# Restacking rotated queries and keys: SBUF-to-SBUF copies replaced by a write to DRAM and a read back

## The chip, the cores and the metric

The kernel runs as one program on 1 core of one Trainium2 chip. The metric is the device time of one execution in microseconds (us). Five engines work side by side, each through its own in-order queue: TensorE (PE, matrix products; PEld is its weight load), VectorE (DVE), ScalarE (ACT), GpSimd (POOL), and SyncE (SP), which here does nothing but issue transfers. The transfers run on 16 DMA engines.

## The reference, cut to what matters

Two requests (x_prompt and x_sample, 512 tokens by 1024 each) go through the same two encoder layers and a last norm. One layer computes:

```
h    = rmsnorm(x) * (1 + scale) + shift          # scale, shift, gate from silu(c) @ w_ada
proj = h @ w_in                                  # 1024 -> qa ka va ga qb kb vb gb
A: 8 heads x 64: rotary q, k; three centred windows (128,1) (512,4) (2048,16),
   merged by their softmax denominators; times silu(ga)
B: 4 heads, key 64, value 128: rotary q, k; two-directional retention with decay,
   RMS norm per head; times silu(gb)
x    = x + gate * (concat(A, B) @ w_out)
```

At 512 tokens every head is one 512 by 512 score matrix with a mask (A) or a decay table (B). Both need `q . k` over the 64 rotated elements of a head, and this is where the change lies.

## The kernel before, in words

**Precision.** A float32 operand is split into a rounded high part and a low part (`hi`, `lo`), and a product is taken as hi·hi + lo·hi + hi·lo. With a head of 64 and 128 rows in the array, q's two parts are stacked on the 128 partitions (a tile QS), and k's high part is stacked twice (KS), its low part twice (KL). One product QS by KS then gives (q_hi + q_lo)·k_hi, a second one QS by KL adds the low part of k.

**Projection and order.** `ITEMS` lists 20 projection items a layer: four of query/key pairs of A (PQK), two of B (RQK), values (PV, RV) and gates (G). The main loop (line 1267) runs through them in that order and issues their products on PE. Everything else is written as generators (tasks) that a planner (`Plan`, line 125) steps through: it keeps a clock for every engine, adds an estimated cost for each instruction, and takes a task's next step when its due time, the value it yields, has come on PE's clock. The planner runs while the program is built; its choices fix the order of every engine's queue. Buffers come from a heap of half tiles (`Heap`), PSUM banks from `Banks`; a step is also held until those it needs are free.

**A turn.** Each query/key item is done once for each request: (4 + 2) items by 2 requests by 2 layers make 24 turns, and a turn holds two heads. `rope` (line 851) does a turn: six DVE operations apply the rotation to two PSUM banks (tiles rc and rs, which hold for both heads the first and the second half of q and k, 32 rows each), ACT rounds the two results to `hi`, DVE subtracts to get `lo`. Then come the copies (lines 868 to 877): for each head four copies into QS, four into KS, four into KL, each of 32 partitions by 2 KB, 64 KB, from SBUF to SBUF. All 24 are one step of the task: nothing else can be put between them on SP. Their due time is 1.5 us before the last source is planned to be ready; the four source tiles are given back after the copies.

**Who uses the stacks.** `attn` (line 911) takes the stacks of an A turn, in turn order: scores on PE, mask and minimum on DVE, `soften` (line 934: exponential on ACT, scaling and splitting into pt on DVE), two DMA transposes a head (pt to pT, line 957, on SP), and the product with the values. `ret` (line 1044) takes those of a B turn: scores, decay on DVE, `halve`, products. The weights (`raw`, line 769) are loaded through the same SP queue, rounded by ACT to wH, and POOL subtracts to get wL.

**The planner's view of a transfer.** `note` (line 159) charges SP 650 ns for an SBUF-to-SBUF copy and 450 ns for one with DRAM (line 421), and lets the bytes run one after the other at a fixed rate. A write into part of a tile (fewer than 128 partitions) does not wait in the plan for the transfer before it into the same tile.

In the traces nearly every instruction has line 377, where the helper records it, so groups are told apart by the names of their tiles. The names rc, rs, th, sS, yr, KL and so on are those of whoever opened the buffer first, so copies into stacks appear also as `QS<-sS` or `sr<-rs`.

Of the kernel before, what the change touches and what calls it, by code (L numbers as in the profile page):

```python
# [10 lines left out]
F32 = mybir.dt.float32  # L11
F32R = mybir.dt.float32r
# [7 lines left out]
P = 128  # L20
# [16 lines left out]
K_STK = 6  # L37
# [87 lines left out]
class Plan:  # L125
# [31 lines left out]
        return 0.0 if t <= self.free[eng] else t  # L157

    def note(self, eng, cost, outs, ins, nbytes=0.0):
        part = eng == "SP" and outs[0].shape[0] < P  # L160
        outs = [k for a in outs for k in self.keys(a)]
        ins = [k for a in ins for k in self.keys(a)]
        start = self.free[eng]
        for k in ins:
            start = max(start, self.seen(eng, self.ready.get(k)))
        for k in outs:
            if not (part and self.last.get(k, (0.0, ""))[1] == "DMA"):
                start = max(start, self.seen(eng, self.last.get(k)))
        if self.dead.intersection(outs + ins):
            raise RuntimeError("use of a spare buffer")  # L170
        end = start + cost
        self.free[eng] = end
        if eng == "SP":
            self.dma = max(end + 650.0, self.dma) + nbytes
            end = self.dma + 770.0
            eng = "DMA"
        for k in outs:
            self.ready[k] = (max(end, self.ready.get(k, (0.0, ""))[0]), eng)
        for k in outs + ins:
            if end >= self.last.get(k, (0.0, ""))[0]:  # L180
                self.last[k] = (end, eng)
# [243 lines left out]
def trunk_kernel(  # L425
# [8 lines left out]
    plan = Plan()  # L434
    V, A, G, T, Q = (Engine(plan, n, e) for n, e in (("DVE", nc.vector), ("ACT", nc.scalar), ("POOL", nc.gpsimd),
                                                     ("PE", nc.tensor), ("SP", nc.sync)))
# [3 lines left out]
    dp = ctx.enter_context(tc.tile_pool(name="dp", bufs=1, space=bass.MemoryType.DRAM))  # L440
# [5 lines left out]
    H = Heap(plan, cp, "half", NHALF)  # L446
# [392 lines left out]
    def main_wide(pj, job, l, b):  # L839
        for t in range(TT):  # L840
            out = pj[:, t // 2, (t % 2) * 256:(t % 2) * 256 + 256]
            for k in range(KT):
# [5 lines left out]
                T.matmul(out, h, wl, start=False, stop=False)  # L848
                T.matmul(out, lo, wh, start=False, stop=(k == KT - 1))

    def rope(pj, c, s, res, b):
        yield lambda: plan.after("DVE", *pj)
        V.tensor_tensor(c[0], pj[0], cos, op=ALU.mult)
        V.tensor_tensor(s[0], pj[0], sin, op=ALU.mult)
        B_IN.free(pj[0])
        V.tensor_tensor(s[1], pj[1], sin, op=ALU.mult)
        V.tensor_tensor(c[0], c[0], s[1], op=ALU.subtract)
        V.tensor_tensor(c[1], pj[1], cos, op=ALU.mult)
        B_IN.free(pj[1])
        V.tensor_tensor(c[1], c[1], s[0], op=ALU.add)  # L860
        for t in (1, 0):
            yield lambda: plan.after("ACT", c[1 - t])
            A.activation(s[t].bitcast(F32R), c[1 - t], AF.Copy)
        hi, lo = (s[1], s[0]), c
        for t in range(2):
            yield lambda: plan.after("DVE", hi[t])
            V.tensor_tensor(lo[t], lo[t], hi[t], op=ALU.subtract)
        yield lambda: max(plan.at(*hi, *lo) - 1500.0, H.avail(1, 6, K_STK, "R"))
        out = []
        for h in range(2):  # L870
            qs, ks, kl = H.take(1, "QS"), H.take(1, "KS"), H.take(1, "KL")
            for i in range(4):
                Q.dma_start(qs[32 * i:32 * i + 32], (hi, lo)[i // 2][i % 2][32 * h:32 * h + 32])
            for t, src in ((ks, hi), (kl, lo)):
                for i in range(4):
                    Q.dma_start(t[32 * i:32 * i + 32], src[i % 2][64 + 32 * h:96 + 32 * h])
            out.append([x.bitcast(F32R) for x in (qs, ks, kl)])
        res["stk"][b] = out
        H.free(*c, *s)

    def turn(kind, i, b, pj, res):
        rs = res.setdefault((kind[0], i), {"stk": {}, "vv": {}})
        c, s = [H.take(1, "rc") for _ in range(2)], [H.take(1, "rs") for _ in range(2)]
        spawn(rope(pj, c, s, rs, b), front=True)
        if kind == "PQK":
            follow(attns, attn(i, b, rs))
# [361 lines left out]
    for l in range(DEPTH):  # L1248
# [8 lines left out]
        for ks in PIECES if l == 0 else ():  # L1257
            for idx in early:
                for t, pj in enumerate(early[idx]):
                    main_half(pj, jobs[idx], t, l, 0, ks)  # L1260
                if KT - 1 in ks:
                    kind, i = ITEMS[0][idx]
# [63 lines left out]
        for b in range(NB):  # L1326
            for t in range(TT):
# [8 lines left out]
                for c, (n0, n1) in enumerate(LAST if final else ((0, D),)):  # L1336
                    for n, k in enumerate(KORDER):
                        pump(lambda: plan.at(*yT[(k, b)], *wo[k]) if (k, b) in yT and k in wo else INF)
                        y, w = ([x.bitcast(F32R) for x in z] for z in (yT[(k, b)], wo[k]))
# [48 lines left out]
```

## Time and profile before

| | us |
|---|---|
| median of 3 runs | 1138.96 (1136.25 to 1142.01) |
| the profiled execution, its own time | 1141.08 |
| its span, first to last instruction | 1139.3 |
| PE busy | 1062.7 (93%) |
| DVE busy | 855.4 (75%) |
| ACT busy | 388.8 (34%) |
| POOL busy | 193.4 (17%) |
| mean granted TensorE clock | 0.973 of full speed |
| DMA, share of 16 engines | 55.0%, 163.55 MB |

Busy time is the sum of an engine's instructions. The span is cut into slices or stretches to see where an engine stands still; the chain of waits says which engine's work ended last at each moment. The 1.8 us between the span and the execution's own time lie outside the first and last instruction. A granted clock of 1.0 is 2.4 GHz, 0.5 is 1.2 GHz.

### The profile page before, as it was taken

Reading aid. Unit: us, or ns where it says so; the run is one execution under the profiler, and the core shown is the slowest. Engines: PE = TensorE matmul, PEld = TensorE weight load, DVE = VectorE, ACT = ScalarE, POOL = GpSimd, SP = SyncE. Lnnn points to the kernel's source line nnn. Section 1 sums busy time; section 2 is a strip of 40 time slices with the busy share of each in tenths; the row PEclk is TensorE's granted clock in tenths of the full one; section 3 lists DMA queues with packets and bytes.
Section 4 is the critical chain, followed back from the end, with each engine's and each line's share of the span. In section 5 each row is a group of like instructions: output and inputs, shape, how many; then the busy total and the mean of one; then the engine's idle time right before and its main releaser. Section 6 shows DMA issues by size and latency. Waiting matters only on the chain.

```text
span 1139.3 us, 15515 instructions
## 1 busy us (share of the span) xinstructions
PE 1062.7 (93%) x5443; PEld 838.8 (74%) x5443; DVE 855.4 (75%) x1664; ACT 388.8 (34%) x677; POOL 193.4 (17%) x84
## 2 busy tenths in 40 slices
PE   5979999999888989999999999999999999976997
PEld 3757787687766557777888878877887887854886
DVE  5577876688747979889447799589956986797555
ACT  6353314233124313454324333424234233334101
POOL 3052002010120201136000101102111012051000
PEclk9989999999989989999999999999999999987999
DMA  9804877316775756778322386336752477664232
GB/s 316 289 24 139 167 177 230 136 48 163 158 173 143 240 123 149 161 178 259 111 74 75 79 181 162 79 93 149 146 128 65 132 149 167 140 212 102 75 111 74
DMA packets 210429, 164.53 MB, mean 144 GB/s; under 512 B 162032, under 2 KB 172560, under 8 KB 210352
## 3 DMA queue, kind: packets, MB, share of 16 engines
q1 hardware_dynamic: 210352, 163.55, 55.0%
q8 instruction: 43, 0.70, 0.3%
q14 instruction: 34, 0.28, 0.1%
HBM read 79.59 MB, written 8.40 MB: 77 GB/s over the span
## 4 chain that ended last, share of the span: by engine, by line
PE 55%; DVE 25%; SPq 10%; DMA 4%; issue 3%; ACT 2%; POOL 0%; DVEq 0%; ACTq 0%; POOLq 0%
PE banks L377 55%; DVE pt L377 10%; SPq L377 10%; DVE sS L377 2%; DVE rc L377 2%; DVE yr L377 2%; DVE sm L377 1%; DVE th L377 1%; DMA wa<-in_w_ada_dram 1%; DVE hT L377 1%; DVE rsq L377 1%; DMA raw<-in_w_in_dram 1%; DVE sd L377 1%; DVE rs L377 1%; DVE b L377 1%
## 5 line engine op out<-in xcount | busy, mean ns | idle before, releaser
L377 PE MATMUL banks<-hT,wH 128*128 128x512 f32 x1536 | 487.3, 398 | 12.1 <-POOL hT L377 4.4
L377 PEld LDWEIGHTS banks<-hT,wH 128*128 128x128 f32 x1536 | 289.6, 191 | 92.0 <-issue 14.5
L377 PE MATMUL banks<-hT,wL 128*128 128x512 f32 x768 | 303.2, 395 | 3.7 <-POOL wL L377 3.7
L377 POOL TENSOR_TENSOR wL<-raw,wH 128x1024 fp32r<-128x1024 f32 x56 | 139.8, 2505 | 744.4 <-ACT wH L377 577.2
L377 PE MATMUL banks<-wo,yT 128*128 128x512 f32 (+1 forms) x744 | 170.7, 390 | 10.1 <-DVE yT L377 6.9
L377 PEld LDWEIGHTS banks<-hT,wL 128*128 128x128 f32 x768 | 146.5, 191 | 35.1 <-POOL wL L377 4.1
L377 PEld LDWEIGHTS banks<-wo,yT 128*128 128x128 f32 x744 | 139.0, 192 | 40.0 <-DVE yT L377 7.6
L377 PE MATMUL banks<-wH,hT 128*128 128x256 f32 x512 | 96.7, 285 | 0.5 <-ACT wH L377 0.5
L377 ACT ACTIVATE sS<-sS,sm 128x512 f32<-128x512 f32 x76 | 54.3, 715 | 88.2 <-DVE sm L377 78.4
L377 PEld LDWEIGHTS banks<-wH,hT 128*128 128x128 f32 x512 | 81.9, 193 | 2.0 <-ACT wH L377 0.7
L377 DVE SCALAR_TENSOR_TENSOR pt<-sS,sm,pt 128x512 f16<-128x512 f32 x76 | 75.5, 993 | 4.2 <-PE banks L377 1.1
L377 PE MATMUL banks<-wL,hT 128*128 128x256 f32 x256 | 73.1, 285 | 2.2 <-POOL wL L377 2.2
L377 ACT ACTIVATE wH<-raw 128x1024 fp32r<-128x1024 f32 x56 | 58.6, 1052 | 36.8 <-PE banks L377 19.0
L377 DVE CUSTOM_DVE_ANT_0 sS<-banks,tabs 128x512 f32<-128x512 f32 x76 | 49.1, 686 | 18.3 <-PE banks L377 15.9
L377 PE MATMUL banks<-sr,rv 128*128 128x512 f32 x166 | 49.1, 402 | 6.1 <-DVE sr L377 4.7
L377 DVE TENSOR_SCALAR pt<-sS,sm 128x512 f16<-128x512 f32 x76 | 51.4, 676 | 1.6 <-DMA KS<-rc 0.2
L377 PEld LDWEIGHTS banks<-wL,hT 128*128 128x128 f32 x256 | 49.4, 193 | 3.2 <-POOL wL L377 2.4
L377 DVE TENSOR_TENSOR res<-banks,gb 128x512 f32<-128x512 f32 (+1 forms) x33 | 22.1, 670 | 39.4 <-PE banks L377 39.4
L377 POOL TENSOR_TENSOR wo<-rawo,wo 128x1024 fp32r<-128x1024 f32 x16 | 41.2, 2596 | 57.6 <-PE banks L377 29.6
L377 PE MATMUL banks<-pT,vn 128*64 128x512 f16 x384 | 45.8, 383 | 1.6 <-DMA pT<-pt 1.1
L377 ACT ACTIVATE sq<-xr 128x1024 bf16<-128x1024 f32 (+2 forms) x15 | 14.2, 944 | 87.9 <-issue 43.2
L377 PE MATMUL banks<-wa,siluT 128*32 128x128 f32 (+1 forms) x384 | 33.0, 406 | 10.9 <-DMA wa<-in_w_ada_dram 7.9
(326 smaller groups left out, 1384.5 us busy)
## 6 DMA issues: line engine op xcount, KB each, us to landing
raw<-in_w_in_dram SPq DMA_DIRECT2D x56, 512.0 KB, 4.3
wa<-in_w_ada_dram SPq DMA_DIRECT2D x48, 512.0 KB, 4.9
rawo<-in_w_out_dram SPq DMA_DIRECT2D x16, 512.0 KB, 4.5
QS<-rs SPq DMA_DIRECT2D x88, 64.0 KB, 2.0
KL<-rc SPq DMA_DIRECT2D x88, 64.0 KB, 2.0
KS<-rs SPq DMA_DIRECT2D x66, 64.0 KB, 2.0
x1d<-xr SPq DMA_DIRECT2D x8, 512.0 KB, 2.8
xr<-x1d SPq DMA_DIRECT2D x8, 512.0 KB, 4.1
```

Source lines behind the costliest of these rows:

```text
L377: r = fn(*args, **kw)
```

## The change

A turn gets a scratch tile of 1 MB in DRAM, 128 rows by (half, part, 512). Each of the four source tiles is written to it whole, 128 partitions by 2 KB, 256 KB, as a step of its own with a due time 0.7 us before that tile is planned to be ready. The four source tiles are given back right after the writes. One more step, due 0.5 us before the scratch is planned to have landed, reads six stacks back, 256 KB each: QS as 128 rows in a run, KS and KL as 64 rows of which each is read twice. The rows of a stack come in another order than before, the same for q and k. In the planner, writes to a scratch tile don't wait for one another.

```diff
     def note(self, eng, cost, outs, ins, nbytes=0.0):
-        part = eng == "SP" and outs[0].shape[0] < P
+        part = eng == "SP" and (outs[0].shape[0] < P or outs[0].tensor.name.startswith("stk"))
...
-        yield lambda: max(plan.at(*hi, *lo) - 1500.0, H.avail(1, 6, K_STK, "R"))
+        nstk[0] += 1
+        rd = dp.tile([P, 2, 2, 512], F32, name=f"stk_dram{nstk[0]}")
+        for i, x in enumerate((*hi, *lo)):
+            yield lambda: plan.at(x) - 700.0
+            Q.dma_start(rd[:, i % 2, i // 2, :], x)
+        H.free(*c, *s)
+        yield lambda: max(plan.at(rd) - 500.0, H.avail(1, 6, K_STK, "R"))
         out = []
         for h in range(2):
-            qs, ks, kl = H.take(1, "QS"), H.take(1, "KS"), H.take(1, "KL")
-            for i in range(4):
-                Q.dma_start(qs[32 * i:32 * i + 32], (hi, lo)[i // 2][i % 2][32 * h:32 * h + 32])
-            for t, src in ((ks, hi), (kl, lo)):
-                for i in range(4):
-                    Q.dma_start(t[32 * i:32 * i + 32], src[i % 2][64 + 32 * h:96 + 32 * h])
-            out.append([x.bitcast(F32R) for x in (qs, ks, kl)])
+            q, k = rd[32 * h:32 * h + 32], rd[64 + 32 * h:96 + 32 * h]
+            srcs = [q.rearrange("p j w n -> (p j w) n")]
+            srcs += [k[:, :, w, :].rearrange("p j n -> (p j) n")[:, None, :].to_broadcast([64, 2, 512]) for w in range(2)]
+            ts = [H.take(1, n) for n in ("QS", "KS", "KL")]
+            for t, x in zip(ts, srcs):
+                Q.dma_start(t, x)
+            out.append([t.bitcast(F32R) for t in ts])
         res["stk"][b] = out
-        H.free(*c, *s)
```

## Rows read from the trace of the kernel before

**Rows 1.** The page, span in 40 slices: busy tenths of PE, DVE; granted clock.

```profile
PE   5979999999888989999999999999999999976997
DVE  5577876688747979889447799589956986797555
PEclk9989999999989989999999999999999999987999
```

**Rows 2.** Stretches: length; busy us of PE, PEld, DVE, ACT, POOL; clock; DMA share; GB/s.

```profile
80.00:280.00 200.00, 197.42 (x986) 152.75 (x985) 144.13 (x262) 58.18 (x106) 29.06 (x12) 0.99 0.55 147
280.00:360.00 80.00, 67.81 (x386) 52.36 (x386) 53.25 (x86) 26.36 (x45) 12.99 (x5) 0.91 0.71 164
360.00:460.00 100.00, 91.59 (x412) 65.51 (x411) 87.70 (x169) 32.87 (x69) 12.79 (x5) 0.95 0.67 172
500.00:520.00 20.00, 17.46 (x78) 13.04 (x74) 19.75 (x16) 11.32 (x16) 15.00 (x6) 0.91 0.70 178
640.00:1000.00 360.00, 355.56 (x1812) 290.81 (x1811) 287.71 (x523) 126.12 (x234) 56.32 (x23) 1.00 0.57 130
1000.00:1040.00 40.00, 22.60 (x94) 16.36 (x93) 38.11 (x50) 18.55 (x33) 19.93 (x8) 0.75 0.68 190
```

**Rows 3.** Chain that ended last, 280 to 360, then 1000 to 1040: shares by line.

```profile
by line: SPq L377 33.1%; PE banks L377 13.2%; DMA pT<-pt 10.1%; issue 6.4%; DVE pt L377 6.0%; DVE sm L377 4.3%; DVE rc L377 4.0%; POOL wL L377 3.6%; DVE sr L377 3.3%; DMA QS<-rc 2.5%; DMA KS<-b 2.4%; DVE yr L377 2.4%; DVE rsq L377 1.7%; DVE
...
by line: DVE pt L377 57.9%; issue 13.8%; DVE sm L377 9.5%; DVE y L377 5.0%; DVE th L377 4.9%; DVE sS L377 4.7%; PE banks L377 2.0%; DVE yT L377 1.5%; DVE rsq L377 1.5%; DVEq L377 0.6%; ACT sS L377 0.5%; DVE yr L377 0.1%; ACTq L377 0.0%
```

**Rows 4.** Timeline of SP: start, duration; the last two turns' copies and what stands between.

```profile
922.48 0.54 SPq L377 DMA_DIRECT2D sr<-rs  x1
...
937.00 0.59 SPq L377 DMA_DIRECT2D KS<-rc  x1
937.68 4.69 SPq L377 DMA_TRANSPOSE pT<-pt  x2
942.55 1.03 SPq L377 DMA_DIRECT2D raw<-in_w_in_dram  x2
944.59 3.40 SPq L377 DMA_TRANSPOSE vn<-vt  x1
948.03 1.21 SPq L377 DMA_DIRECT2D sr<-rs  x2
```

**Rows 5.** Timeline of DVE: a pt half done, and the last turn's rotation done.

```profile
926.57 0.75 DVE L377 SCALAR_TENSOR_TENSOR pt<-yr,sm,pt 128x512 f16<-128x512 f32 x1
...
933.19 1.29 DVE L377 TENSOR_TENSOR rc<-rc,rs 128x512 f32<-128x512 f32 x2 [1.40 <-ACT rs L377]
```

**Rows 6.** Transfers into QS: SP time min/median/max ns, first and last start; us to landing.

```profile
L377 SPq DMA_DIRECT2D QS<-rs x88: 507/588/1932, 76.2 to 960.8; - x88
...
DMA to landing us min/median/max: 1.9/2.0/6.0
```

**Rows 7.** The same for the 512 KB writes to a DRAM scratch and reads from it.

```profile
L377 SPq DMA_DIRECT2D x1d<-xr x8: 326/326/327, 534.5 to 611.2; - x8
L377 SPq DMA_DIRECT2D xr<-x1d x8: 319/376/423, 1022.0 to 1117.0; - x8
...
DMA to landing us min/median/max: 2.8/3.4/4.4
```

**Rows 8.** The same for outputs, 256 KB twice among nine.

```profile
L377 SPq DMA_DIRECT2D out_dram<-res x9: 337/338/382, 1062.8 to 1136.0; - x9
...
DMA to landing us min/median/max: 2.9/3.1/3.4
```

**Rows 9.** The same for the transposes of pt.

```profile
L377 SPq DMA_TRANSPOSE pT<-pt x64: 1679/2408/4582, 105.3 to 1039.6; - x64
...
DMA to landing us min/median/max: 4.3/5.0/6.5
```

**Rows 10.** Stretches: copies alone; then the last two 256 KB writes to DRAM alone.

```profile
262.00:270.00 8.00, 8.00 (x37) 6.64 (x36) 4.11 (x14) 3.63 (x9) 0.00 (x0) 1.00 0.44 105
...
1136.00:1137.00 1.00, 0.00 (x0) 0.00 (x0) 0.00 (x0) 0.00 (x0) 0.00 (x0) 0.67 0.57 215
1137.00:1138.00 1.00, 0.00 (x0) 0.00 (x0) 0.00 (x0) 0.00 (x0) 0.00 (x0) 0.50 0.83 309
```

**Rows 11.** Timeline of SP and chain, 298 to 350: copies, loads behind them, a product's wait.

```profile
308.10 0.59 SPq L377 DMA_DIRECT2D KS<-rc  x1
308.79 1.03 SPq L377 DMA_DIRECT2D raw<-in_w_in_dram  x2
...
308.79 1.14 DMA raw<-in_w_in_dram
318.37 2.91 POOL wL L377
...
341.78 1.93 DMA KS<-b
```

**Rows 12.** Timeline of DVE: two pt operations of one kind in the last stretch.

```profile
1006.51 0.75 DVE L377 SCALAR_TENSOR_TENSOR pt<-sS,sm,pt 128x512 f16<-128x512 f32 x1
...
1013.54 2.71 DVE L377 SCALAR_TENSOR_TENSOR pt<-sS,sm,pt 128x512 f16<-128x512 f32 x1
```

More of the change, by code (lines that the diff above doesn't have):

```diff
@@ L849, in main_wide @@
                 T.matmul(out, lo, wh, start=False, stop=(k == KT - 1))
+    nstk = [0]
     def rope(pj, c, s, res, b):
```

## The prediction

> **What bounds the kernel now.** First the page's slices [rows 1]: PE is at nine tenths or more in most of them, so the span is a full PE with holes, and the question is which holes belong to the copies. The table of stretches [rows 2] says where they are. I count a hole as PE's idle time plus what the lower granted clock takes, at most (1 - clock) times the stretch, an upper bound because the mean clock also covers idle time. 280 to 360: 80 - 67.8 = 12.2 idle and 0.09 x 80 = 7.2 of clock, 19.4 together. 360 to 460: 8.4 + 5.0 = 13.4. 500 to 520: 2.5 + 1.8 = 4.3. 640 to 1000: 4.4, clock 1.00. 1000 to 1040: 17.4 + 10.0 = 27.4. Sum 68.9 us: that is all the change can win, since before 80 us no turn is copied but for a few issues, and after 1040 there are no turns.
>
> Then the chain of waits in the two worst stretches [rows 3]. In 280 to 360 SP's queue holds 33% of it, the transposes behind it 10%, PE 13%: this stretch belongs to SP. In the timeline [rows 11] the last copy of a turn goes out at 308.10, the weight load right behind it at 308.79, and POOL's wL, for which PE then waits, comes only at 318.4; at 341.78 a copy itself is what the chain waits on. DVE is not the cause there: busy 53.3 of 80. In 360 to 460 it is (87.7 of 100). In 1000 to 1040 DVE's pt holds 58% and SP nothing, DVE is busy 38.1 of 40. There DVE also runs slowly: POOL is busy 19.9 of 40 [rows 2], and the same pt operation takes 2.71 us in place of 0.75 [rows 12].
>
> **What the change removes, adds and moves.** Removed: 24 copies a turn at 0.59 us (median) on SP. In the timeline [rows 4] one turn runs from 922.48 to 937.00 + 0.59 = 937.59: 15.1 us, 0.63 a copy with the gap. With the landing of 2.0 [rows 6] a stack is complete 17.1 us after its first copy. 24 turns hold SP for 24 x 15.1 = 362 us.
>
> Added: 4 writes at 0.33 us [rows 7, 8] = 1.3 us, a wait for the last one to land, and 6 reads at 0.38 [rows 7] = 2.3 us. Both issue times are of transfers of 128 partitions with DRAM on one side, as these are. The landing of 256 KB is not shown alone; from below it is 2.0, the 64 KB copy; from above 4.4, the slowest 512 KB to or from scratch [rows 7], and 6.0 where other transfers are queued ahead [rows 6]. I take 3.0, the nine outputs [rows 8], two of which are of just this size. So SP is held 1.3 + 3.0 + 2.3 = 6.6 us a turn (5.6 to 9.6), and 8.5 are freed, 24 x 8.5 = 204 us of SP. The plan may put other issues into the wait; I count none. Behind the waiting read stand SP's next issues: weights, transposes, the next turn's writes; for these wait ACT's wH, then POOL's wL, then PE, and the products with the values. They stood behind 15.1 us of copies before.
>
> The stack: all four sources ready, the last write 0.3, landing 3.0, six reads 2.3, landing of the last 4.0 (between 3.0 and 4.4, six together being more than one): 9.6 us in place of 17.1, so 7.5 earlier.
>
> The bytes grow from 24 x 64 KB = 1.57 MB to 10 x 256 KB = 2.62 MB a turn. What that costs the 16 engines: copies alone move 105 GB/s at a share of 0.44, 239 at full share; writes of 2 KB rows to DRAM move 215 at 0.57 and 309 at 0.83, 375 at full share [rows 10]. So 6.6 us of the engines' time before and 7.0 after if the reads run like the writes, 11.0 if they run like the copies. I take 7.0, DRAM rows of the same length; at 11.0 the share grows by 24 x 4.4 / 1139 = 9 points over 55, most of it where transposes also run.
> The Trainium skill (DMA: Bandwidth & Descriptors, Specifications) has transfers at line rate from 512 B a row on, with a ceiling of 435 GB/s. By that both kinds would cost the same per byte, 3.6 us before and 6.0 after, an estimate from that page. It would add 2.4 us a turn beside the transposes and take perhaps a third of the gain, 1118; the trace does not agree, its copies stay at 239.
>
> Moved: source buffers come free after the writes, some 10 us sooner, and a turn holds six halves of the heap at its reads where it held ten. Cost nothing; a gain only where a projection waits for buffers, which I don't count. Each write is its own step, and waits on SP at most the planned 0.7 us for ACT or DVE; the one step before waited up to 1.5. No cost either way. DVE, ACT, POOL and PE keep all their instructions, and the weight products keep their order; where scores and DVE work stand among them the plan will change.
>
> **The sum**, by stretches. 280 to 360: SP is the chain, and it shrinks to less than half of its length; DVE has 27 us idle there. Two thirds of 19.4, 13. 360 to 460: DVE-bound, but some of its work can move forward into those 27 idle us; half of 13.4, 7. 500 to 520: the same, half, 2. 640 to 1000: half, 2. 1000 to 1040: worked from the last two turns [rows 4, 5]. The last rotation ends at 933.2 + 1.3 = 934.5, its first copy goes out at 948.0, 13.5 later, because SP was in the turn before until 937.6 and then in two transposes, a load and another transpose (10.4 us). The pt half ready at 927.3 was transposed at 937.7. With 6.6 in place of 15.1 for the turn before, the last one starts at 948.0 - 8.5 = 939.5 and is complete 9.6 + 1.0 later, 950 in place of 948.0 + 15.9 + 2.0 = 966. That is 16 us, in which DVE is a fifth idle (287.7 of 360), and it lets the last scores spread out. But POOL's subtractions stay beside the end. Half of 27.4, 14.
> Gain 13 + 7 + 2 + 2 + 14 = 38. Against it 4 us for a new hole: a new order of queues makes one somewhere, and PE lost 12.2 in a stretch of three or four of them, so 3 to 4 each. 1141.1 - 34 = 1107 against the profiled execution's own time; the median of the runs lies 2.1 below that: **1105**.
>
> **Rivals.**
> *All holes go*: SP was behind the DVE-bound stretches too, since late stacks made DVE idle first and full afterwards (53 of 80, then 88 of 100). For: this order of the stretches. Against: the POOL contention at the end, and the holes' clock part is an upper bound. 1141.1 - 68.9 - 2.1 = 1070. Chance 0.10.
>
> *The round trip is slow*: writes land behind transposes and weight loads in the same engines, and the in-order SP stands. Price: both landings at the 6.5 of the slowest transpose [rows 9]: held 1.3 + 6.5 + 2.3 = 10.1, stack complete after 0.3 + 6.5 + 2.3 + 6.5 = 15.6, so 5.0 of 8.5 and 1.5 of 7.5 remain. Some 40% of the 38 is left, 15: 1124. For: transposes and turns stand side by side [rows 4]. Against: scratch transfers never took over 4.4. It reaches 15.1, no gain, only at a landing of 11.5. Chance 0.14.
> The Trainium skill (DMA: Bandwidth & Descriptors, Latency and other measured facts) puts an access of HBM at 0.2 us and 2 us at high load, and calls its write receipt the slowest. By it a landing would be 3.0 + 1.8 = 4.8 under load, an estimate, and the time about 1113. The scratch rows (2.8 to 4.4) partly bear it out.
>
> *Hidden anyway*: the stretch 640 to 1000 has turns back to back and PE lost 4.4 in 360. If 280 to 360 only hands its holes on to DVE, full from 370 on, and the end stays with POOL, nothing is left: 1139. Chance 0.13.
>
> *Slower, by DVE's order*: stacks that come earlier put scores, masks and pt into DVE's in-order queue ahead of the rotations and gates that give PE its projection banks back. Place: 360 to 460, where DVE has 12 us to spare, and the turns of 760 to 840 in layer 1. It decides if more than those 12 us of attention move in there: then PE stands as it does at 1000 to 1040. Price: one more hole of 27.4 against a gain in 280 to 360 alone: 1141.1 + 27.4 - 13 - 2.1 = 1153. For: PE's waits inside full-DVE stretches exist already. Against: a score step is held while DVE's planned clock is more than 3 us ahead of PE's. Chance 0.16.
>
> **Numbers.** Forecast 0.47 (1090 to 1120), all holes 0.10, slow round trip 0.14, hidden 0.13, slower 0.16. Half a per cent, 5.7 us, is what a measurement of this kernel can tell from no change. Faster: 0.47 + 0.10 + 0.13 of the slow round trip = 0.70. Same: 0.13 + 0.01 = 0.14. Slower 0.16. Range: half of all holes lies below 1078; of the slower case half lies above 1148; 1078 to 1148 leaves out about 0.13, and I keep it, since the 27.4 may come in part only.
>
> **What would show it.** Right: SP's issues of a turn 3.6 us with a wait of 2 to 4 between writes and reads; landings under 4.4; SP's share of the chain in 280 to 360 under 15%, PE over 73 of 80 there; the last stack before 955, and PE idle near 9 in the last 40 us before the output products. Wrong: reads that wait over 6 us on SP; a DMA share over 64%; PE holes released by DVE in places where there were none; the end still 17 idle with DVE full, which would say that the stacks were not what made it late.

## The result, and the profile after

The changed kernel takes 1149.79 us (median; 1147.15 to 1152.69), the kernel before beside it 1137.61 (1135.54 to 1142.01). The ratio is 1.0102, 95% interval 1.0062 to 1.0143: slower by 1%, and outside the range 1078 to 1148. The forecast was 1105.

The profiled execution took 1148.95 us, its span is 1147.2. PE is busy 1063.2 us, the same as before, at a mean clock of 0.969 (before 0.973), so nearly all of the 7.9 us of longer span is PE idle time. The page's slices, PE and the granted clock, of after:

```profile
PE   5989999989999899925999999998999898999997
...
PEclk9979999999999999966999999999999999999999
```

Against [rows 1], the dips at 280 to 360 and at 1000 to 1040 are gone, and there is one at 490 to 540 that was not there. The same stretches as in [rows 2], with the same columns (busy us of PE, PEld, DVE, ACT, POOL; clock; DMA share; GB/s), of after:

```profile
80.00:280.00 200.00, 191.57 (x953) 142.85 (x951) 148.56 (x261) 60.31 (x110) 31.81 (x13) 0.98 0.69 192
280.00:360.00 80.00, 80.00 (x483) 62.44 (x482) 58.71 (x98) 27.22 (x44) 9.66 (x4) 1.00 0.77 217
360.00:460.00 100.00, 96.93 (x446) 76.12 (x445) 86.27 (x151) 32.79 (x60) 19.62 (x8) 0.98 0.77 203
460.00:540.00 80.00, 46.94 (x188) 32.90 (x188) 60.16 (x94) 28.15 (x54) 25.29 (x10) 0.75 0.52 127
640.00:1000.00 360.00, 347.87 (x1760) 283.15 (x1759) 306.33 (x552) 130.47 (x243) 57.38 (x23) 0.99 0.61 167
1000.00:1040.00 40.00, 38.95 (x195) 29.87 (x194) 28.39 (x40) 13.30 (x22) 15.34 (x7) 1.00 0.67 158
```

The fourth, of before, which [rows 2] show only in its part 500 to 520:

```profile
460.00:540.00 80.00, 77.46 (x367) 59.90 (x366) 71.31 (x106) 33.54 (x56) 34.32 (x13) 0.98 0.77 202
```

So PE gained 12.2 us in 280 to 360, 5.3 in 360 to 460 and 16.4 in 1000 to 1040, 33.9 together, nearly the 34 that the forecast wanted of these three stretches (13, 7 and 14). The stop at 1000 to 1040 has not just moved on: in 1040 to 1110 PE is busy all 70 us, before and after. It lost 30.5 in 460 to 540, 7.7 in 640 to 1000 and 5.9 in 80 to 280, 44.1 together. The balance is -10.2; the rest of the span gave 2 to 3 us back. In 460 to 540 the clock fell from 0.98 to 0.75 as well. The question is what stands at the end of layer 0. PE's timeline there (start, duration, instruction; in brackets the idle time before it and what ended it), of after:

```profile
431.26 0.39 PE L377 MATMUL banks<-KL,QS 128*128 128x512 f32 x1
...
475.63 0.39 PE L377 MATMUL banks<-QS 128*128 128x512 f32 x1
...
504.31 2.08 PE L377 MATMUL banks<-KS,KL 128*128 128x512 f32 x4 [16.40 <-DVE sS L377]
```

PE computes no score from 431.26 to 475.63, and stands still for 16.4 us when DVE has to take the scores one by one. Were the stacks late? SP's timeline of the same kernel:

```profile
430.39 0.90 SPq L377 DMA_DIRECT2D rawo<-in_w_out_dram  x2
...
439.96 1.21 SPq L377 DMA_DIRECT2D KS<-stk_dram  x2
```

They were not: the last read of that turn is issued by 441.2, and reads land in about 5 us, so the stack is there at some 446 and waits 29 us for its first score. The first line shows something else that is new: the loads of the output weights (rawo) begin at 430.39, thirty microseconds sooner than in the kernel before, whose first one is

```profile
460.22 0.53 SPq L377 DMA_DIRECT2D rawo<-in_w_out_dram  x1
```

The stretch in slices of 10 us, of after:

```profile
450.00:460.00 10.00, 10.00 (x57) 7.01 (x56) 2.23 (x2) 1.77 (x3) 2.38 (x1) 1.00 0.91 250
460.00:470.00 10.00, 10.00 (x46) 8.28 (x45) 2.76 (x4) 0.71 (x2) 0.00 (x0) 1.00 0.18 72
470.00:480.00 10.00, 10.00 (x44) 7.88 (x43) 5.09 (x14) 3.17 (x7) 0.00 (x0) 1.00 0.52 157
480.00:490.00 10.00, 7.91 (x35) 6.20 (x34) 9.68 (x16) 8.78 (x15) 6.48 (x3) 1.00 0.57 211
490.00:500.00 10.00, 0.00 (x0) 0.00 (x0) 9.89 (x6) 1.76 (x3) 10.00 (x5) 0.65 0.00 0
```

DVE (the third busy number) is idle for two thirds of 450 to 480, the time in which the held scores could have given it work. Then it is full, does 6 instructions in 10 us where it did 16, and POOL is busy without a gap: most of that is its subtractions for the output weights (five of the seven from 483.5 to 501.4; the other two are for projection weights). First DVE is starved, then it gets everything at once beside POOL.

**The theory** formed from this: the new order takes heap buffers too early. A score step needs two buffers and must leave `K_SS` = 6 (line 926). The output weights (`load_o`, started when `LATE` = 5 items are left, line 1281) take theirs from the heap as soon as `K_RAWO` = 12 and `K_WO` = 10 allow. Turns that finish sooner add stacks that wait. Sources freed after the writes made room just where the weights look for it. The scores are what goes without. **Rivals**: the transfers themselves do it (a slow round trip, 25 MB more traffic); or it is chance, any new order of this kernel costs or gains some per cent.

### The profile page after: what moved, and what is told of

It is laid out like the page before. It is cut to its first block, busy times and chain, and to the rows that moved or that the text cites. A ratio compares the mean times of both kernels' runs of the same rounds, so it can differ in the third digit from the quotient of the medians.

```text
span 1147.2 us, 14865 instructions
## 1 busy us (share of the span) xinstructions
PE 1063.2 (93%) x5443; PEld 840.6 (73%) x5443; DVE 861.7 (75%) x1664; ACT 391.1 (34%) x678; POOL 191.9 (17%) x84
## 4 chain that ended last, share of the span: by engine, by line
PE 56%; DVE 31%; DMA 7%; issue 3%; SPq 2%; ACT 1%; POOL 0%; DVEq 0%; POOLq 0%; ACTq 0%
PE banks L377 56%; DVE pt L377 9%; DVE rsq L377 3%; DVE sS L377 3%; DMA wa<-in_w_ada_dram 2%; DVE sd L377 2%; DVE sm L377 2%; SPq L377 2%; DVE rc L377 2%; DVE hT L377 1%; DVE rs L377 1%; DVE yr L377 1%; DVE nw L377 1%; DMA stk_dram<-rc 1%; DMA KL<-stk_dram 1%
## 5 line engine op out<-in xcount | busy, mean ns | idle before, releaser
L377 PE MATMUL banks<-wo,yT 128*128 128x512 f32 (+1 forms) x792 | 179.1, 387 | 6.0 <-DVE yT L377 5.5
L377 PEld LDWEIGHTS banks<-wo,yT 128*128 128x128 f32 x792 | 146.5, 190 | 37.3 <-DVE yT L377 5.9
L377 ACT ACTIVATE sS<-sS,sm 128x512 f32<-128x512 f32 x84 | 60.0, 716 | 99.5 <-DVE sm L377 99.1
L377 DVE SCALAR_TENSOR_TENSOR pt<-sS,sm,pt 128x512 f16<-128x512 f32 x84 | 83.5, 994 | 3.5
L377 DVE CUSTOM_DVE_ANT_0 sS<-banks,tabs 128x512 f32<-128x512 f32 x84 | 54.3, 686 | 13.6 <-PE banks L377 13.4
L377 PE MATMUL banks<-pT,vn 128*64 128x512 f16 x384 | 50.4, 410 | 11.8 <-DMA pT<-pt 10.6
L377 DVE TENSOR_SCALAR pt<-sS,sm 128x512 f16<-128x512 f32 x84 | 55.2, 658 | 3.4 <-PE banks L377 1.8
L377 PEld LDWEIGHTS <-vn 128*64 128x64 f16 x384 | 23.3, 116 | 36.3 <-issue 20.9
L377 PE MATMUL banks<-KS,KL 128*128 128x512 f32 x96 | 28.5, 414 | 18.3 <-DVE sS L377 16.4
```

Source lines behind the costliest of these rows:

```text
L377: r = fn(*args, **kw)
```

## The experiments

Each ran in three rounds beside the kernel before (1137.3 to 1137.4 us); ratios are to that.

**The transfers alone.** The queues keep the order of before: the planner is charged for the 24 copies, and the four writes and six reads go out in their place.

```diff
-        for i, x in enumerate((*hi, *lo)):
-            yield lambda: plan.at(x) - 700.0
-            Q.dma_start(rd[:, i % 2, i // 2, :], x)
-        H.free(*c, *s)
+        yield lambda: max(plan.at(*hi, *lo) - 1500.0, H.avail(1, 6, K_STK, "R"))
+        for i, x in enumerate((*hi, *lo)):
+            nc.sync.dma_start(rd[:, i % 2, i // 2, :], x)
...
+                note_copy(qs[32 * i:32 * i + 32], (hi, lo)[i // 2][i % 2][32 * h:32 * h + 32])
```

> The ten DRAM transfers, issued where the 24 copies stood, while the planner goes on charging 24 copies: every queue keeps the order of the kernel before. Order theory (transfers are cheaper as forecast, the loss comes from what the new plan lets happen at the end of layer 0): faster than before, 1118 to 1132, PE near 75 of 80 in 280 to 360. Transfer theory (the round trip itself, landings of 5 us and 60% more bytes, is what costs): 1143 to 1155, as in the changed kernel.

1134.52 us, 0.9968 [0.9954, 0.9982]: the transfers are worth 0.3%, and they make no new hole. Stretches of this kernel:

```profile
280.00:360.00 80.00, 72.47 (x421) 56.60 (x421) 58.99 (x97) 29.56 (x50) 12.56 (x5) 0.96 0.75 195
460.00:540.00 80.00, 77.60 (x367) 59.80 (x366) 71.24 (x115) 33.43 (x55) 33.16 (x12) 0.98 0.75 209
1000.00:1040.00 40.00, 22.42 (x84) 15.84 (x83) 38.45 (x54) 18.35 (x34) 15.14 (x6) 0.70 0.70 167
```

The end of layer 0 is as before, so the loss there comes with the order. Only 4.7 of the 12.2 us in 280 to 360 come with the transfers: PE's 72.47 and the total both say less for them than had been expected. And the hole at the end of layer 1 is untouched (22.4 of 40), although the last stack is read by 944.8 here:

```profile
944.12 0.69 SPq L889 DMA_DIRECT2D KL<-stk_dram  x1
```

With a landing of 5 that is the 950 which the prediction had asked for. So in the old order a stack that lands sooner does not close that hole (more on it below).

**Scores before weights, in two ways.** One number in the changed kernel; and, by itself, the sources freed where they were freed before.

```diff
-K_SS = 6
+K_SS = 4
```

> The changed kernel with one number changed: a score step may start when 4 half tiles would be left to others instead of 6 (K_SS). Order theory: the scores of the last pair of layer 0 are no longer held for buffers, PE's hole of 16.4 us at 488 to 504 and those up to 537 go, 1112 to 1128. Transfer theory: the hole may move, the time stays at 1143 to 1152.

```diff
-        H.free(*c, *s)
         yield lambda: max(plan.at(rd) - 500.0, H.avail(1, 6, K_STK, "R"))
...
         res["stk"][b] = out
+        H.free(*c, *s)
```

> The changed kernel, with the four source tiles given back after the reads are issued, as before the change, and not right after the writes. Order theory: the output weights find fewer free buffers, are loaded later, and the hole at the end of layer 0 shrinks to under 8 us; 1110 to 1130. Transfer theory: 1143 to 1152, the early release was a help if anything.

1129.89 us, 0.9926 [0.9898, 0.9954], and 1129.86, 0.9926 [0.9899, 0.9953]: each takes 20 us off the changed kernel, and the 16.4 us stop is gone in both. `K_SS` is read at one place, the score step, so it was the heap that held that step. The first total is 2 us above what was expected of it, the second within. The pair's scores follow their stack at once; PE's timeline of the first, then of the second:

```profile
447.73 0.50 PE L377 MATMUL banks<-QS 128*128 128x512 f32 x1
```

```profile
446.70 0.50 PE L377 MATMUL banks<-QS 128*128 128x512 f32 x1 [3.11 <-DVE th L377]
```

About half of the loss stays, as one stop for DVE's yT (13.2 and 11.2 us, more than the 8 expected of the second) beside POOL's subtractions; PE in 460 to 540 is at 62.8 and 64.6.

**Control: the same number in the kernel before**, where the scores are not held.

> Control: the kernel before with K_SS 4 instead of 6. In its trace no score of layer 0 waited long for a buffer. Both theories: within 6 us of before, 1131 to 1143; if it gains as much as the changed kernel does with the same number, the number alone, not the hold at the end of layer 0, is what helps.

A miss: 1166.13 us, 1.0244 [1.0215, 1.0272]. It opens holes of its own, the first of them at the same layer end:

```profile
520.01 1.12 PE L377 MATMUL banks<-small,th 128*128 128x128 f32 x4 [15.89 <-DVE th L377]
```

So the rival of chance is alive: a number of the planner moves this kernel by 29 us for reasons of its own, and one run that gets faster by 20 proves no cause. What speaks for the theory is that two different edits close the same stop at the same place, by letting the same scores go. The next pair asks from the other side.

**Weights later, and weights earlier in the kernel before.** `LATE` from 5 to 3 in the changed kernel, and `K_RAWO` from 12 to 4 in the one before, which lets the weights take buffers there as the new order does here.

> The changed kernel with the output weights loaded and split two projection items later (LATE 3 instead of 5). Buffer theory (output weights and waiting stacks fill the heap, so the last pair's scores of layer 0 are held): hole at 488 to 504 gone, 1118 to 1132. Rival (DVE is what ends layer 0 late and the heap only says so): within 6 us of the changed kernel, 1143 to 1155.

> The kernel before, its 24 copies kept, with output weights allowed into the heap down to 4 half tiles left (K_RAWO 4 instead of 12). Buffer theory: the loss of the changed kernel can be made without the change, the last pair of layer 0 waits for buffers and the end of layer 0 comes 10 to 25 us later, 1147 to 1165. Rival: the heap is not what counts, within 6 us of before, 1131 to 1143.

1133.15 us, 0.9952 [0.9931, 0.9972], and 1181.23, 1.037 [1.0331, 1.0409]. With later weights 17 us of the changed kernel come back (1 us less than expected; the stop before the scores is gone, one of 12.8 us for DVE's yT stays). Earlier ones cost the kernel before 44 us, 16 more than expected at most, without any change in the stacks. The stretch of this second kernel; the start of the last turn's copies in SP's timeline of before and of this kernel; and the first score after them in this kernel:

```profile
460.00:540.00 80.00, 58.68 (x260) 43.14 (x260) 63.45 (x84) 27.07 (x45) 33.20 (x13) 0.86 0.66 174
```

```profile
465.17 1.21 SPq L377 DMA_DIRECT2D KL<-rs  x2
```

```profile
484.00 1.17 SPq L377 DMA_DIRECT2D QS<-rs  x2
494.42 0.39 PE L377 MATMUL banks<-QS 128*128 128x512 f32 x1
```

The place is the same, PE short by 21 us with DVE not full (63 of 80), but it is another step that goes late: the whole last turn, whose copies start 19 us later than before, and not its scores, which follow the copies at once. And the stretch holds only 18.8 of the 44 us; another 20 are lost at the end of layer 1, where PE is busy 50.0 of the 70 us from 1040 to 1110. No transfer was changed here, so a loss of this kind needs no slow transfer; that the transfers make none in the changed kernel, the first run showed. That this stretch is easily upset the control above shows too; what the theory adds is the sign: the three edits that give to the scores or take from the weights win in the changed kernel, and the one that gives to the weights loses in the old one. The control is the exception: it gives to the scores in the old kernel, where they were not held, and loses 29 us.

**The subtraction off POOL.** The second way above, and the output weights' low part computed on DVE.

```diff
-                    G.tensor_tensor(t.bitcast(F32R), raw, out[0], op=ALU.subtract)
+                    V.tensor_tensor(t.bitcast(F32R), raw, out[0], op=ALU.subtract)
```

> As the kernel with the late release, and the 16 subtractions of the output weights (2.5 us each on POOL) done by DVE. Collision theory: in the last 50 us of a layer POOL's subtractions stretch DVE's pt operations from 0.5 or 0.75 to 2.5 and more, some 18 us a layer; on DVE they cost 16 x 1.1 = 18 us in all, so 36 - 18 less DVE time at the two ends, 1108 to 1124. Rival (the holes at the layer ends have another cause): 1127 to 1140.

1121.91 us, 0.9849 [0.9817, 0.9881], 8 us better than without, and PE in 460 to 540 goes from 64.6 to 74.3: what is left of the hole at the layer's end is mostly POOL beside DVE.

**All numbers together, and in the kernel before.**

```diff
-LATE = 5
+LATE = 3
...
-K_SS = 6
+K_SS = 4
...
-K_WO = 10
+K_WO = 14
...
-K_RAWO = 12
+K_RAWO = 20
```

> The changed kernel with four numbers changed so that output weights and their splits come later and scores go first (LATE 3, K_SS 4, K_RAWO 20, K_WO 14). Buffer theory: no score of either layer waits for buffers, PE's holes at the end of layer 0 under 12 us, 1112 to 1126. Rival: like the kernels with one number changed, 1127 to 1133, since what is left there is DVE's own work.

> Control: the kernel before, 24 copies, with the same four numbers (LATE 3, K_SS 4, K_RAWO 20, K_WO 14). If the freed SP queue is what these numbers turn into time, they do little here: 1130 to 1150. If the numbers alone are the gain, 1115 to 1125, as with the changed kernel.

Four numbers are changed. 1119.68 us, 0.9824 [0.9783, 0.9865], and in the kernel before 1142.55, 1.0044 [1.0029, 1.006]. The stretch, of the first and then of the second:

```profile
460.00:540.00 80.00, 75.79 (x347) 58.97 (x347) 68.73 (x108) 32.61 (x54) 29.01 (x11) 0.98 0.64 178
```

```profile
460.00:540.00 80.00, 63.86 (x302) 45.96 (x301) 66.81 (x108) 33.88 (x64) 31.71 (x13) 0.89 0.79 201
```

With numbers that hold the weights back and let the scores go, the new hole is gone but for some 4 us. The control says that the numbers are no gain in themselves. At equal numbers the change is worth 1142.55 - 1119.68 = 22.9 us, 2.0%; with the old numbers it is worth -12.2. But the four numbers were found on the changed kernel, and one of them, `K_SS` 4, by itself costs the old one 29 us. Against the old kernel with its own numbers (1137.3) the gain is 17.7 us, 1.6%; which numbers would suit the old kernel best was not asked.

**The best version**: these numbers and the subtraction on DVE; and the same with the planner told that a read from the scratch lands 1.7 us later, as it does.

> The changed kernel with the four numbers, and the 16 subtractions of the output weights on DVE. Collision theory: POOL's stretching of DVE at the layer ends (21 and 13 us in the trace with the four numbers) goes for 18 us of own work, and the end of layer 0 no longer waits for it: 1108 to 1118. Rival (nothing left to win at the ends): 1117 to 1124.

> As the last one, with the planner told that a read from the scratch lands 1.7 us later than it thought (5.0 us were measured, some 3.3 planned). Landing theory: PE's waits on stacks (0.8 to 2.5 us each, 8 us together in the trace with the four numbers) go, 5 to 8 us less than the last one. Rival: the plan puts other products in between that it would have done later anyway, within 3 us of it.

1112.07 us (1104.83 to 1114.21), 0.976 [0.972, 0.98], and 1112.14, 0.9775 [0.9735, 0.9816]. The first beats both kernels, by 25 us the one before and by 38 the changed one; the truer landing adds nothing. The subtraction on DVE was not tried in the kernel before, so not all of the 25 are shown to be the change's. At the layer's end of the first:

```profile
460.00:540.00 80.00, 80.00 (x375) 63.50 (x375) 64.41 (x128) 34.72 (x57) 8.78 (x3) 1.00 0.67 187
```

## Why the prediction was wrong, by its own steps

**SP's queue: right.** In 280 to 360 SP is gone from the chain of waits, where it held a third [rows 3]. The chain's shares by line, of after:

```profile
by line: PE banks L377 100.6%
```

The prediction wanted PE over 73 of 80 there, and it is 80.00. The transfers alone give 4.7 of the 12.2 us; the rest comes with the new order, also where the sources are freed late (79.8 of 80).

**The price of a turn: too low, and it did not decide.** One turn in SP's timeline of after:

```profile
651.24 1.66 SPq L377 DMA_DIRECT2D stk_dram<-rs  x2
653.00 0.87 SPq L377 DMA_DIRECT2D stk_dram<-rc  x2
656.67 0.92 SPq L377 DMA_DIRECT2D QS<-stk_dram  x2
...
658.92 1.17 SPq L377 DMA_DIRECT2D KS<-stk_dram  x2
```

It holds SP for 660.1 - 651.2 = 8.9 us, not 6.6 and not the 15.1 of [rows 4]. The page gives the landings (KB each, median us):

```profile
QS<-stk_dram SPq DMA_DIRECT2D x48, 256.0 KB, 4.8
KL<-stk_dram SPq DMA_DIRECT2D x44, 256.0 KB, 5.2
stk_dram<-rs SPq DMA_DIRECT2D x41, 256.0 KB, 3.4
stk_dram<-rc SPq DMA_DIRECT2D x24, 256.0 KB, 4.0
```

Writes were taken at 3.0 and the last read at 4.0; they measure 3.4 to 4.0 and 4.8 to 5.2. The forecast's 9.6 us counted from the last write; by this turn and the landings it is some 11 (13 from the first write), and still sooner than the 17.1 of the copies. A read's issue takes 0.52 to 0.60 us (median), not the 0.38 of the 512 KB reads [rows 7]. PE waits for the reads in all 4.9 us in the changed kernel. The DMA share rose by 3.3 points: 0.583 x 1147.2 - 0.550 x 1139.3 = 42 us over 24 turns, 1.8 a turn on top of the 6.6, between the two bounds of 7.0 and 11.0.
The Trainium skill (DMA: Bandwidth & Descriptors, Latency and other measured facts) puts an access of HBM at 0.2 us, and at 2 us at high load. From that the prediction had estimated 4.8 for a landing under load, beside the sum. The reads agree with it; the writes into DRAM, at 3.4 to 4.0, lie below, so here it was the reads out of DRAM that took longer.

**"Moved: ... Cost nothing; a gain only where a projection waits for buffers": the step that failed.** It asked who gains from buffers that come back early, and named one taker. There are others, and the heap gives to whoever asks first. The output weights took the room at 430, the scores, which must leave six, got none until 475, and the layer's end, where DVE was already full (500 to 520 in [rows 2]), got all their work at once. The price was 30.5 us of PE and a clock of 0.75 there. Moving that one line back gives 20 us (1129.86), and the same room guarded by numbers 30 (1119.68). The prediction did say that "the plan will change", and counted 4 us for it.

The forecast was short by 44.8 us. 30 of them go with the numbers that say who may take buffers (20 by moving that one line back alone); some 15 are not put down to a step. Part of them is the 5.9 us lost in 80 to 280 and the 7.7 in 640 to 1000, where the forecast had 0 and a gain of 2: PE is no better there in the kernel with four numbers (191.72 and 346.45). In the changed kernel about 9 of them are three stops of some 3 us in which PE waits for DVE's nwr; why these came was not taken apart. Of the prediction's own signs of being wrong, the one that came was a stop for DVE where there had been none, the 16.4 us above.

**1000 to 1040: the right size for a wrong reason.** The forecast wanted 14 there because the last stack would come 16 us sooner. In the changed kernel it comes later by the clock, its reads going out until 973.5 where copies went out until 960.8 [rows 6], and the stop is gone; with the old order and the stack at 950 it stays. By PE's work, of which the changed kernel has done 24 us less by 1000, the stack is some 9 us sooner. But in neither kernel do the scores come at once: complete at some 966 before and 979 after, the last stack has its scores from about 989.5 on in both, after in one go until 995.8, before in pieces until 1023.5. PE's timeline of before, then of after:

```profile
1018.24 0.79 PE L377 MATMUL banks<-QS 128*128 128x512 f32 x1 [7.30 <-DVE sm L377]
```

```profile
993.53 2.27 PE L377 MATMUL banks<-KS,KL 128*128 128x512 f32 x8 [1.29 <-DVE sm L377]
```

So it was not the stack that they waited for; what held them before, no run shows. The reads into KS of after, the source of the 973.5 (SP time min/median/max ns, first and last start):

```profile
L377 SPq DMA_DIRECT2D KS<-stk_dram x48: 513/596/1077, 87.5 to 973.5; - x48
```

What also differs is when DVE works. Stretches of before, then of after:

```profile
960.00:980.00 20.00, 20.00 (x89) 16.35 (x88) 13.71 (x35) 8.39 (x19) 2.62 (x1) 1.00 0.56 132
1000.00:1020.00 20.00, 12.70 (x53) 10.19 (x52) 19.56 (x23) 7.38 (x11) 12.42 (x5) 0.84 0.71 210
```

```profile
960.00:980.00 20.00, 16.82 (x71) 12.87 (x70) 18.59 (x42) 8.92 (x20) 2.39 (x1) 1.00 0.93 286
1000.00:1020.00 20.00, 20.00 (x89) 16.36 (x88) 15.15 (x26) 6.72 (x13) 5.33 (x2) 1.00 0.72 151
```

Before, DVE had a third of 960 to 980 free and then too much beside POOL; after, it is full 40 us earlier, at a price of 3.2 us of PE there, part of the 7.7 lost in 640 to 1000. Why the new order came out so was not taken apart further.

**The rivals.** *Slower, by DVE's order* had a chance of 0.16 and its price, one more hole of 27.4 us, was about right (30.5). Its mechanism was not: at the end of layer 0 attention did not push ahead of other DVE work, it was held back. Whether the three new stops for nwr are of its kind is open. *The round trip is slow* is ruled out by the transfers alone, which are 0.3% faster. *Hidden anyway* nearly holds in the old order, where the transfers are worth 0.3%, but not in the new one, by the 22.9 us between two kernels with equal numbers (17.7 against the old kernel with its own). What no rival held was that the planner's margins had been set for an SP that was late.

**What stays open.** How much of a gain or a loss of one of these kernels is the theory and how much is luck of the order: a control with one number (1166.13) shows that luck can be worth 29 us. For single kernels only the holes named above are explained.

## What to carry to other kernels

When an edit gives a resource back sooner, list everything that is waiting to take it, in the order in which it may, and ask who then goes without; "free sooner" is a change of order and costs nothing only if nobody else asks. A scheduler's margins belong to the delays that they were set with: when a delay goes, test the change with the margins set again, and give the old kernel the same margins as a control. To tell a transfer's price from that of the order it brings, run the new transfers in the old order.

## What the runs showed of the hardware

POOL's subtraction delays many of DVE's operations by most of its own length. DVE's timeline of after, beside POOL's at the same time:

```profile
494.20 2.71 DVE L377 SCALAR_TENSOR_TENSOR pt<-sS,sm,pt 128x512 f16<-128x512 f32 x1
...
496.83 0.15 DVE L377 RECIPROCAL sm<-sm 128x2 f32<-128x2 f32 x1
497.01 2.11 DVE L377 TENSOR_SCALAR sm<-sm 128x2 f32<-128x2 f32 x1
...
501.72 0.75 DVE L377 SCALAR_TENSOR_TENSOR pt<-th,sm,pt 128x512 f16<-128x512 f32 x1
```

```profile
493.84 5.26 POOL L377 TENSOR_TENSOR wL<-raw,wH 128x1024 fp32r<-128x1024 f32 x2
499.07 2.33 POOL L377 TENSOR_TENSOR wo<-rawo,wo 128x1024 fp32r<-128x1024 f32 x1
```

Even an operation on two columns takes 2.11 us while POOL runs, though not every one: the reciprocal just before it, on the same two columns, takes 0.15. At 501.7, when POOL is done, the pt operation is back at 0.75.
The Trainium skill (SBUF — State Buffer, Who interferes with whom) has the port pair that the two engines share as an exclusive lock, held for a whole instruction, in which the loser waits; the rows agree: 2.71 against 0.75 for the pt operation, and 2.11 for two columns, are both about 2 us more, most of a POOL instruction of 2.3 to 2.6, whatever the DVE operation's own size.

The subtraction itself is cheaper on DVE, 1.2 us (1217 ns) in the best version, than the 2.54 that it takes on POOL. In 460 to 540 the yT operations come back with it. Of the best version,

```profile
L377 DVE TENSOR_TENSOR wo<-rawo,wo 128x1024 fp32r<-128x1024 f32 x8 | 9.7, 1217 | 0.0
L377 DVE TENSOR_TENSOR yT<-th,yT 128x512 fp32r<-128x512 f32 x3 | 2.0, 683 | 0.0
```

and of the same numbers with the subtraction on POOL,

```profile
L377 DVE TENSOR_TENSOR yT<-th,yT 128x512 fp32r<-128x512 f32 x4 | 9.1, 2324 | 0.0
```

The pt operations, at 1143 ns in the changed kernel, are back at 752 with the four numbers alone, by which they no longer run beside POOL. Eight subtractions there cost DVE 9.7 us, and the whole change of engine gave 7.6 us (1119.68 to 1112.07).
